# Blocks of 80 rows, 5 for each DMA engine, in place of 64 rows and 4, in a column roll of 8192 x 8192 floats

## Chip, cores, metric

One core of one Trainium2 chip. The metric is the device time in microseconds (us). A profile is a separate execution; its span is about 1.8 us shorter than the time of the same execution (815.4 and 817.17, 838.7 and 840.44). All ratios below are those of the record, worked out from fast runs of the same rounds on one chip, so they are not quite the ratio of the medians quoted beside them; the plain means of the listed runs give the same within 0.001. Intervals are 95%.

## The reference

```python
def setup_inputs():
    return {"x": np.random.randn(8192, 8192).astype(np.float32), "shift": 100}

def reference(x, shift):
    return np.roll(x, shift, axis=1)
```

Nothing is computed. Each row of 32 KiB moves 100 columns to the right, and the last 100 columns come to the front.

## The kernel before

A row is cut in two. The **long piece**, output columns 128 to 8191, is 8064 floats or 32,256 bytes, and goes straight from HBM (the chip's main memory) to HBM. The **head piece**, output columns 0 to 127, goes through on-chip memory; GpSimd issues it, and the change does not touch it.

```python
engines = [nc.sync, nc.scalar]
...
xm = x.rearrange("(c e j) w -> j e c w", e=16, j=4)
om = out.rearrange("(c e j) w -> j e c w", e=16, j=4)
depth = n_rows // 64 // 4
for c in range(4):
    for j in range(4):
        if a < n_cols:
            cs = slice(c * depth, (c + 1) * depth)
            engines[j % 2].dma_start(out=om[j, :, cs, a:], in_=xm[j, :, cs, g:n_cols - s])
...
for k, h in enumerate(tiles):          # head pieces, after loads and copies
    for q in range(Q):
        nc.gpsimd.dma_start(out=ot[k, q, :, :, :a], in_=h[:, q])
```

In a copy `j` is fixed, `e` is the outermost dimension and deals the rows to the 16 DMA engines (the traces list the queue of a packet, not its engine), and `c` steps from block to block. Row `64c + 4e + j` is engine `e`'s. So neighbouring engines stand 4 rows or 128 KiB apart (I call this the **pitch**), and an engine's next row in the same copy lies 64 rows or 2 MiB further on (the block step). SyncE and ScalarE each issue 8 such copies, 32 rows deep for each engine.

## Time and profile before

| | before |
|---|---|
| median of the timed runs | 828.96 us (828.69 to 829.57) |
| span of the profiled execution | 815.4 us |
| bytes read plus written in HBM | 536.9 MB |
| busy time of VectorE, GpSimd | 3.7 us, 16.1 us |
| shortest, median hold of one long row by an engine (470 to 800 us) | 1.19, 1.53 us |

No compute engine matters. The useful number is one that the page does not print for a stretch: the HBM traffic. The prediction works it out from the megabytes of the DMA queues and shows the lines. (q1 and q10 are the two hardware queues, q0 is the software queue.)

### The profile page before, as it was taken

How to read it: one execution, taken by the hardware profiler on the slowest of the kernel's cores; microseconds unless marked ns; L12 is line 12 of the kernel's file. 1: busy time of each engine (PE TensorE's matmuls, PEld its weight loads, DVE VectorE, ACT ScalarE, POOL GpSimd, SP SyncE). 2: the span in 40 equal slices, each digit the busy share in tenths (PEclk: the TensorE clock that was granted, in tenths of full speed). 3: DMA queues.
4: the chain of work that ended last, by engine and by line, in shares of the span. 5: the costliest groups of instructions: out<-in, count | busy, mean ns of one | idle time of the engine just before them, and what ended most of it. 6: DMA issues, size and time to landing. Idle time of an engine off the chain costs nothing. (4 is left out here: it accounts for less than half of the span.)

```text
span 815.4 us, 93 instructions
## 1 busy us (share of the span) xinstructions
DVE 3.7 (0%) x4; POOL 16.1 (2%) x22
## 2 busy tenths in 40 slices
DVE  0000000000000000000000000000000000000000
POOL 3000001000010000000000000000000000000000
DMA  9999999999999999999999999999999999999996
GB/s 310 341 328 347 330 349 335 337 340 346 338 337 346 338 348 348 347 333 345 340 344 337 349 326 335 334 329 334 335 329 331 329 335 334 332 331 332 329 334 250
DMA packets 10784, 272.63 MB, mean 334 GB/s; under 512 B 544, under 2 KB 544, under 8 KB 2592
## 3 DMA queue, kind: packets, MB, share of 16 engines
q10 hardware_dynamic: 4224, 132.12, 47.0%
q1 hardware_dynamic: 4224, 132.12, 46.9%
q0 software_dynamic: 2336, 8.39, 4.5%
HBM read 268.44 MB, written 268.44 MB: 658 GB/s over the span
## 5 line engine op out<-in xcount | busy, mean ns | idle before, releaser
L76 POOL DMA_DIRECT2D out_dram<-h x8 | 6.9, 954 | 170.1 <-DMA h<-in_x_dram 144.1
L67 POOL DMA_DIRECT2D t<-in_x_dram x6 | 5.4, 910 | 0.8 <-PEq L107 0.8
L69 DVE COPY h<-t 128x2400 f32<-128x2400 f32 x2 | 2.8, 1410 | 208.5 <-DMA t<-in_x_dram 208.5
L71 POOL DMA_DIRECT2D h<-in_x_dram x2 | 1.8, 883 | 28.6 <-DMA t<-in_x_dram 28.6
L68 POOL DMA_DIRECT2D h<-in_x_dram x2 | 1.8, 882 | 27.0 <-DMA t<-in_x_dram 27.0
L72 DVE COPY h<-t 128x672 f32<-128x672 f32 x2 | 1.0, 503 | 0.0
L93 POOL MEMSET const-float32-0.0<- 128x1 f32 x1 | 0.1, 99 | 0.2 <-issue 0.2
L93 POOL MEMSET const-bfloat16-1.0<- 128x1 bf16 x1 | 0.1, 103 | 0.0
L93 POOL MEMSET const-float32-1.0<- 128x1 f32 x1 | 0.1, 99 | 0.0
L93 POOL MEMSET const-uint8-127<- 128x1 uint8 x1 | 0.1, 99 | 0.0
## 6 DMA issues: line engine op xcount, KB each, us to landing
out_dram<-in_x_dram SPq DMA_DIRECT2D x8, 16128.0 KB, 401.3
out_dram<-in_x_dram ACTq DMA_DIRECT2D x8, 16128.0 KB, 400.5
out_dram<-h POOLq DMA_DIRECT2D x8, 512.0 KB, 182.5
t<-in_x_dram POOLq DMA_DIRECT2D x6, 512.0 KB, 118.2
h<-in_x_dram POOLq DMA_DIRECT2D x2, 400.0 KB, 151.3
h<-in_x_dram POOLq DMA_DIRECT2D x2, 112.0 KB, 146.1
```

The costliest lines, as they stand in the source:

```text
L67: nc.gpsimd.dma_start(out=t[:, q - 1], in_=lead)
L68: nc.gpsimd.dma_start(out=h[:, Q - 1, :, :s], in_=xt[k, Q - 1, :, :, n_cols - s:])
L69: nc.vector.tensor_copy(h[:, :Q - 1, :, :s], t[:, :, :, :s])
L71: nc.gpsimd.dma_start(out=h[:, 0, :, s:], in_=xt[k, 0, :, :, :g])
L72: nc.vector.tensor_copy(h[:, 1:, :, s:], t[:, :, :, s:])
L76: nc.gpsimd.dma_start(out=ot[k, q, :, :, :a], in_=h[:, q])
L93: nc = _bacc.Bacc("TRN2", target_bir_lowering=False, num_devices=1)
```

## The change

The likely intent: engines and blocks at steps that are no power of two, so that the 16 streams do not fall on the same parts of HBM. The block grows to 80 rows, the pitch to 160 KiB and the block step to 2.5 MiB. As 8192 is not a multiple of 80, 32 rows are left for one more copy; and as 5 is odd, copies fall to the two queues by a running number.

```diff
-    xm = x.rearrange("(c e j) w -> j e c w", e=16, j=4)
-    om = out.rearrange("(c e j) w -> j e c w", e=16, j=4)
-    depth = n_rows // 64 // 4
-    for c in range(4):
-        for j in range(4):
+    V = 5
+    blocks = n_rows // (16 * V)
+    top = blocks * 16 * V
+    xm = x[:top].rearrange("(c e j) w -> j e c w", e=16, j=V)
+    om = out[:top].rearrange("(c e j) w -> j e c w", e=16, j=V)
+    n = 0
+    for c0 in range(0, blocks, 26):
+        for j in range(V):
             if a < n_cols:
-                cs = slice(c * depth, (c + 1) * depth)
-                engines[j % 2].dma_start(out=om[j, :, cs, a:], in_=xm[j, :, cs, g:n_cols - s])
+                cs = slice(c0, min(c0 + 26, blocks))
+                engines[n % 2].dma_start(out=om[j, :, cs, a:], in_=xm[j, :, cs, g:n_cols - s])
+                n += 1
+    if top < n_rows and a < n_cols:
+        nc.sync.dma_start(out=out[top:, a:].rearrange("(c e) w -> e c w", e=16),
+                          in_=x[top:, g:n_cols - s].rearrange("(c e) w -> e c w", e=16))
```

## The prediction

> **What bounds the kernel now.** I read the page's header and its 40 slices first, then its DMA queues, then the chain, then the table of stretches and the DMA view of two stretches.
>
> ```profile
> span 815.4 us, 93 instructions
> DMA  9999999999999999999999999999999999999996
> DMA packets 10784, 272.63 MB, mean 334 GB/s; under 512 B 544, under 2 KB 544, under 8 KB 2592
> q10 hardware_dynamic: 4224, 132.12, 47.0%
> q1 hardware_dynamic: 4224, 132.12, 46.9%
> q0 software_dynamic: 2336, 8.39, 4.5%
> HBM read 268.44 MB, written 268.44 MB: 658 GB/s over the span
> another core or an unknown queue 24%; DMA 4%; POOL 1%; issue 0%; POOLq 0%; PEldq 0%
> ```
>
> The reader is to see that the DMA engines are 90% busy or more in every slice but the last, that the two hardware queues (the long row pieces, issued from SyncE and ScalarE) hold 94% of the engines' time, and that the chain of waits is of no use here: it names the GpSimd side, which the timeline shows issuing its last transfer at 241.7 us of 815, and the long copies never appear in it. So the limit is the transfers. The question is which part of them: the 16 engines, or the HBM that they read and write. Busy engines do not decide it, because an engine that waits for memory counts as busy. Two stretches do, one with all three queues and one with the long pieces alone:
>
> ```profile
> DMA packets 6394, 141.06 MB, mean 341 GB/s; under 512 B 385, under 2 KB 385, under 8 KB 2259
> q10 hardware_dynamic: 2129, 66.61, 46.3%
> q1 hardware_dynamic: 2134, 66.77, 45.1%
> q0 software_dynamic: 2131, 7.68, 8.4%
> ...
> DMA packets 3498, 109.57 MB, mean 332 GB/s; under 512 B 101, under 2 KB 101, under 8 KB 101
> ```
>
> A long piece goes HBM to HBM, so each byte is read and written there; a head piece has one end in on-chip memory and counts once. From 10 to 424 us that gives 2 x (66.61 + 66.77) + 7.68 = 274.4 MB in 414 us, 663 GB/s. From 470 to 800 us it is 2 x 109.57 = 219.1 MB in 330 us, 664 GB/s. The mix differs, the engines' rate differs (341 and 332 GB/s), the HBM rate does not. Now the end:
>
> ```profile
> core 0: us, DVE busy (x) POOL busy (x), PEclk, DMA share, GB/s
> ...
> 470.00:800.00 330.00, 0.00 (x0) 0.00 (x0) 1.00 0.99 332
> 800.00:806.00 6.00, 0.00 (x0) 0.00 (x0) 1.00 0.79 323
> 806.00:812.00 6.00, 0.00 (x0) 0.00 (x0) 1.00 0.59 253
> 812.00:815.40 3.40, 0.00 (x0) 0.00 (x0) 1.00 0.07 28
> ```
>
> While all engines work, one moves 332 / (0.99 x 16) = 21.0 GB/s. With 21% of their time gone an engine moves 323 / (0.79 x 16) = 25.6, and with 41% gone 253 / (0.59 x 16) = 26.8. Losing a fifth of the engines cost 3% of the rate. The packet records say the same: a 32,256 byte row holds its engine 1193 ns at the least (27.0 GB/s), 1534 ns in the median of 470 to 800 us, and 1194 ns for every row that starts after 806 us. So an engine could do a row in 1.19 us, and 512 rows in 611 us; it takes longer because together they run into about 664 GB/s of reads plus writes. **That plateau is the bound.** The whole sum: 536.9 MB / 664 GB/s = 808.5 us, plus about 7 us of beginning and end at a lower rate, is the span of 815.4; the timed 828.96 lies 13.6 us above the span.
>
> **What the Trainium skill says.** "DMA: Bandwidth & Descriptors", section "Specifications", gives about 27 GiB/s for one engine and 716 GB/s for an HBM stack. The fastest rows here (27.0 GB/s) lie somewhat below the first, and 664 is 93% of the second, so the trace agrees that HBM is nearly full. The same page, "Latency and other measured facts", row "HBM row pitch at large powers of two", has copies between HBM tensors at 207 GB/s for a pitch of 512 KiB, 164 for 2 MiB and 103 for 4 MiB, and about 214 once 4 KiB is added; it calls channel aliasing an inference. This is the likely reason for the change. The pitch between engines is 4 rows x 32 KiB = 128 KiB now and 160 KiB after, between blocks 2 MiB and 2.5 MiB. The trace doesn't show such a loss: 329 GB/s in each direction is above the page's undisturbed figure. Section "Issuing engines are not separate DMA queues" says that SyncE and ScalarE feed the same engines; the trace agrees, since both queues move 132.12 MB in the same time. "Why a DMA increments its semaphore by 16 and not by 1" takes the number of engines of a copy from the outermost dimension, 16 here before and after.
>
> **The change, part by part.**
> 1. Bytes and rows: none is added. 8192 = 102 x 80 + 32, so an engine gets 102 x 5 + 2 = 512 rows, as before 128 x 4 = 512. Rows stay whole packets of 32,256 bytes. Worth 0 us.
> 2. Issues: 20 copies and a tail of 32 rows in place of 16. Each adds 16 completion records of 4 bytes; the records show 9 ns for one. 5 more are 80 records, 5 per engine, 0.05 us. An issue's own time lies beside running transfers: an issuing instruction of some 84 us is one that waits for room. A copy is 26 rows deep for each engine in place of 32, so the eight in flight still leave each engine 78 or more rows in its two queues. Worth under 0.1 us.
> 3. Share of the queues: SyncE takes even numbers and the tail, (3+2+3) x 26 + 2 x 24 + 2 = 258 rows for each engine; ScalarE (2+3+2) x 26 + 3 x 24 = 254. ScalarE's queue ends 4 rows earlier. A row alone on an engine took 1194 ns after 806 us, so a single queue fills it. Worth 0 to 1 us.
> 4. The uneven end: from 800 us on the engines run out one after another, the stretches above hold 323 x 6 + 253 x 6 + 28 x 3.4 = 3.55 MB, which 332 GB/s would move in 10.7 us of the 15.4. So 4.7 us is all that a perfect end could give. Today engine e always sits at the same offset modulo 2 MiB (e x 128 KiB plus j rows); after the change the offsets wander with the block, so a lasting disadvantage of one engine may even out. I estimate 0 to 3 us of gain.
> 5. Address pattern, the purpose: if banks or channels collide because of the fixed offsets, the plateau rises. Everything else stays. I estimate +0 to 0.5% of rate, 0 to 4 us.
> Sum: 829 - 1.5 - 2 + 0.5 = 826 us.
>
> **The rivals.**
> First, **aliasing is real** and the new pitch lifts the plateau. 2% of time needs 16.6 us, so a rate of 664 x 808.5 / 791.9 = 678 GB/s, 95% of the stack's figure; at 690 the time would be 829 - 30 = 799. For it: 77 to 85% of the rows take longer than the 1.21 us of an undisturbed one, and reads and writes at like offsets could meet in one bank. Against it: collisions should slow rows also below the plateau, but at 646 GB/s (800 to 806 us) an engine reached 95% of its own best rate, and the plateau was the same at 10 us, with the engines just started in step, as at 700 us, where they have drifted apart. It does not refute a loss tied to the fixed offsets, for those do not change with drift.
> Second, **the fixed offsets were an advantage**: 16 engines at 16 different multiples of 128 KiB never share one; wandering offsets coincide by chance. If the plateau fell by 3% to 644, the span's 808.5 would become 834 and the time 854. Nothing in the trace speaks for it beyond the neat layout.
> Third, **a copy or queue runs dry**, through unequal copies of 24 and 26 rows or the tail behind the last. It would cost at most the 4 rows, 4 x 1.2 = 5 us, time 834. The depth in flight speaks against it.
> Fourth, the engines become the bound: not with a row at 1.19 us where 1.53 is the median.
>
> **Range and chances.** Most likely nothing that matters moves: the bound is bytes through HBM and the bytes stay. A plateau between 655 and 677 makes 840 and 813; with the end and the queues, 810 to 840 should hold it 8 times in 10. Faster by over 2% (under 812.4) needs a plateau above 678, near the stack's figure: 0.12. Slower by over 2% (over 845.5) needs one below 651: 0.08. Within 2%: 0.80.
>
> **What would show it.** Queue of SyncE about 133.2 MB in 258 x 16 + 11 x 16 = 4304 packets, of ScalarE 131.1 MB in 4224; landing of a long copy near 401 x 26 / 32 = 326 us, since eight are in flight either way; head pieces as before. Step 5 is right if bytes counted as above give 660 to 668 GB/s in the middle of the span; step 4 if the last 15 us hold more than 3.55 MB. The prediction is wrong if that rate leaves 651 to 678, or if the hardware queues show engines idle in the middle.

## The result and the profile after

| | before | after |
|---|---|---|
| median, same rounds | 828.83 us (4 runs) | 841.08 us (4 runs) |
| ratio | | 1.0151 [1.0128, 1.0175] |
| span of the page | 815.4 us | 838.7 us |

The change costs 1.5%. That is within 2%, which had a chance of 0.80, but 1 us above the range. A warning first: the two pages lie 23.3 us apart and the timed runs only 12.3. The page of before is of an execution of 817.17 us, while its timed runs took about 829. Later rounds explain the kind of difference: on four chips the same kernel took 818 to 822 us in the median, on a fifth 832. So these two pages give the place of the loss, but its size has to come from kernels run on one chip (runs e1 and e2 below).

The header, the DMA lines and the HBM line of the page after:

```profile
span 838.7 us, 98 instructions
DMA  9999999999999999999999999999999999999996
GB/s 297 327 325 329 321 328 332 324 327 334 341 316 337 340 331 330 335 336 327 340 339 335 323 322 318 326 326 326 323 326 317 328 323 328 320 325 325 329 317 252
DMA packets 10864, 272.63 MB, mean 325 GB/s; under 512 B 624, under 2 KB 624, under 8 KB 2672
q10 hardware_dynamic: 4224, 131.09, 47.3%
q1 hardware_dynamic: 4304, 133.15, 47.0%
q0 software_dynamic: 2336, 8.39, 4.4%
HBM read 268.44 MB, written 268.44 MB: 640 GB/s over the span
```

The bytes are the same, the engines are as busy, and the rate is lower in nearly every slice. Neither queue runs dry. Packets and megabytes of the two queues are those of the prediction's third step. The same two stretches of the DMA view as in the prediction, first 10 to 424 us, then 470 to 800 us, each with its queues (packets, MB, share of 16 engines):

```profile
DMA packets 6207, 136.74 MB, mean 330 GB/s; under 512 B 385, under 2 KB 385, under 8 KB 2198
q10 hardware_dynamic: 2066, 64.58, 46.7%
q1 hardware_dynamic: 2072, 64.74, 44.8%
q0 software_dynamic: 2069, 7.43, 8.3%
...
DMA packets 3452, 106.87 MB, mean 324 GB/s; under 512 B 137, under 2 KB 137, under 8 KB 139
```

The first holds 2 x (64.58 + 64.74) + 7.43 = 266.1 MB in 414 us, 643 GB/s, where before had 663. The second holds 2 x 106.87 = 213.7 MB in 330 us, 648 GB/s, where before had 664. **The plateau itself is lower**, by 3.1% and 2.5%. At 648 GB/s the 536.9 MB take 828.5 us in place of 808.5, 20 of the 23.3 us between the two pages.

The end, from the table of stretches of the kernel after (length, VectorE, GpSimd, clock, DMA share, GB/s):

```profile
core 0: us, DVE busy (x) POOL busy (x), PEclk, DMA share, GB/s
823.30:829.30 6.00, 0.00 (x0) 0.00 (x0) 1.00 0.85 296
829.30:835.30 6.00, 0.00 (x0) 0.00 (x0) 1.00 0.54 231
835.30:838.70 3.40, 0.00 (x0) 0.00 (x0) 1.00 0.11 47
```

The last 15.4 us hold 296 x 6 + 231 x 6 + 47 x 3.4 = 3.32 MB, worth 10.3 us at 324 GB/s, so 5.1 us are lost where before lost 4.7. The end neither gave nor took anything that counts.

### The profile page after: what moved, and what is told of

It is laid out like the page before. It is cut to its first block, busy times and chain, and to the rows that moved or that the text cites. A ratio compares the mean times of both kernels' runs of the same rounds, so it can differ in the third digit from the quotient of the medians.

```text
span 838.7 us, 98 instructions
## 1 busy us (share of the span) xinstructions
DVE 3.7 (0%) x4; POOL 16.1 (2%) x22
```

## Experiments

The theory that I formed from this: **the address pattern of the 5-row blocks lowers the rate that HBM gives** (A), either because an engine's offset now wanders from block to block (A1) or because of the 160 KiB pitch itself (A2). The rival: the new form of issuing, more and shallower copies and another deal to the queues (B). In all kernels the head pieces are unchanged. Only the lines of the long pieces are shown.

### Which part of the change

**e1**: the changed code with 4 rows for each engine.

```diff
-    V = 5
+    V = 4
```

> Blocks of 64 rows and 4 for each engine as before, but issued by the changed code: copies 26 and 24 deep in place of 32, 20 of them, queues taken in turn by a running number. Theory A (the address pattern of 5 rows lowers the plateau of HBM traffic): time within 0.4% of the kernel before, ratio 0.996 to 1.004. Rival B (the shallower copies, their number and the way they fall to the two queues): ratio 1.010 to 1.018, like the changed kernel.

Measured: 820.75 us against 818.48, ratio 1.0023 [1.0001, 1.0045].

**e2**: the changed kernel again, on the same chip and in the same rounds.

> The changed kernel itself, to have it on the same chip and in the same rounds as its variants. All theories: ratio 1.013 to 1.018 to the kernel before, plateau of reads plus writes near 648 GB/s between 470 and 800 us. If it comes out under 1.008, the 1.5% depended on the chip or on where the arrays lay.

Measured: 832.66 us, ratio 1.0173 [1.0145, 1.0200]. B is out: the issue form is worth about 0.2%, the 5 rows about 1.5%. (e1 has no tail copy of 32 rows; neither has e3 below, which loses as much as e2, so the tail is not the cause.) The DMA view of 470 to 800 us, first of e1, then of e2:

```profile
DMA packets 3529, 109.51 MB, mean 332 GB/s; under 512 B 134, under 2 KB 134, under 8 KB 134
```

```profile
DMA packets 3490, 108.45 MB, mean 329 GB/s; under 512 B 128, under 2 KB 128, under 8 KB 128
```

Doubled and divided by 330 us: 663.7 and 657.3 GB/s, 1.0% less, and not the 648 that e2's expectation gave. The earlier stretch, 10 to 424 us, is worse. Its queues (packets, MB, share of 16 engines), first of e1, then of e2:

```profile
q10 hardware_dynamic: 2139, 66.54, 46.6%
q1 hardware_dynamic: 2148, 66.71, 45.2%
q0 software_dynamic: 2143, 7.72, 8.2%
```

```profile
q10 hardware_dynamic: 2098, 65.58, 46.8%
q1 hardware_dynamic: 2103, 65.54, 44.6%
q0 software_dynamic: 2097, 7.54, 8.4%
```

The sums are 274.2 and 269.8 MB in 414 us, 662 and 652 GB/s, 1.6% less. The two losses make 414 x 1.6% = 6.7 us and, over the remaining 390 us, 3.8 us: 10.5 of the 12.7 us between their spans (815.7 and 828.4).

**e3**: pitch still 5 rows, but a copy steps 320 rows (10 MiB), so an engine keeps its offset modulo 2 MiB within a copy. 192 rows go in four small copies of the old form.

```diff
-    xm = x[:top].rearrange("(c e j) w -> j e c w", e=16, j=V)
+    xm = x[:8000].rearrange("(c o e j) w -> o j e c w", o=4, e=16, j=5)   # out likewise; one copy for each (o, j)
```

> Pitch between engines still 5 rows (160 KiB), but each copy steps 320 rows (10 MiB, a multiple of 2 MiB) instead of 80, so an engine keeps its offset modulo 2 MiB within a copy, as in the kernel before; 192 rows are left to four small copies of the old form. Theory A1 (offsets that wander by block let engines that have drifted apart meet at the same offset): the loss goes, ratio 0.995 to 1.005. Theory A2 (the 160 KiB pitch between the engines itself): ratio stays 1.012 to 1.020.

Measured: 835.11 us, ratio 1.0205 [1.0185, 1.0224]. Holding the offset in place does not give the loss back. A1 as the whole cause falls. (The step of 10 MiB is tried in no other run; that it costs nothing of itself is not shown.)

**e4**: blocks of 80 rows, but the first 64 dealt 4 to an engine and the last 16 one to an engine.

```diff
-    xm = x[:top].rearrange("(c e j) w -> j e c w", e=16, j=V)
+    xb = x[:8160].rearrange("(c b) w -> c b w", b=80)                      # out likewise
+    x4 = xb[:, :64].rearrange("c (e j) w -> j e c w", j=4)                 # j = 0..3
+    x1 = xb[:, 64:].rearrange("c e w -> e c w")                            # the fifth copy
```

> Blocks of 80 rows stepped by 2.5 MiB as in the changed kernel, but within the block the first 64 rows are dealt 4 to an engine (pitch 128 KiB) and the last 16 rows one to an engine. Theory A1 (wandering block offsets): ratio 1.012 to 1.020, like the changed kernel. Theory A2 (the pitch between engines): four fifths of the copies run as before, ratio 1.000 to 1.006. Rival B: 1.010 to 1.018.

Measured: 825.13 us, ratio 1.0077 [1.0053, 1.0100], between the two expectations. With e3 it speaks for A2: with most of the old pitch back, more than half of the loss is gone. What is left is not cleared up. e1 gives 0.2% to the issue form, and a fifth of the 0.9% that e11 below finds for a pitch of one row is another 0.2%; the other 0.4% may be the wandering step. On the page of e4 the rate is 657 GB/s from 10 to 424 us and again from 470 to 800 us: what came back, against e2, came back in the first stretch only.

### The pitch varied

**e5 to e8**: the changed code with other numbers of rows.

```diff
-    V = 5
+    V = 8     # e5;  3 in e6, 2 in e7, 6 in e8; copies 32, 29, 32 and 29 deep
```

> 8 rows for each engine, blocks of 128: pitch between engines 256 KiB, again a power of two. Theory A2a (the engines do best when their offsets agree modulo a large power of two): within 0.5% of the kernel before. Rival A2b (the wider the pitch the worse): at least as slow as with 5 rows, ratio 1.015 to 1.04. Aliasing as I had it in the prediction: slower than 4 rows too.

> 3 rows for each engine, blocks of 48 and a tail of 32 rows: pitch 96 KiB, not a power of two but narrower than before. A2a: ratio 1.010 to 1.025, like 5 rows. A2b: 0.99 to 1.00, faster than or like 4 rows.

> 2 rows for each engine, blocks of 32: pitch 64 KiB. A2a with a bound at 128 KiB: slower, ratio 1.005 to 1.02. A2a for any power of two: ratio within 0.5% of 1. A2b: 0.985 to 1.00.

> 6 rows for each engine, blocks of 96 and a tail of 32 rows: pitch 192 KiB = 3 x 64 KiB. A2a: ratio between those of 4 and 5 rows or like 5 rows, 1.005 to 1.02. A2b: 1.017 to 1.03, above 5 rows.

Measured, against 821.82 us in the same rounds: 8 rows 822.78 us, 1.0027 [0.9998, 1.0057]; 3 rows 828.64 us, 1.0096 [1.0069, 1.0124]; 2 rows 823.47 us, 1.0037 [1.0005, 1.0070]; 6 rows 826.41 us, 1.0072 [1.0034, 1.0109]. "The wider the worse" is out: 8 rows beat 3. The powers of two lie within 0.4%, the others lose 0.7 to 1.0%, but the intervals of 2 and 6 rows overlap. In these kernels the block step changes with the pitch (it is 16 times the pitch); e3 and e4 move the one without the other.

**e11 and e12**: two pitches that tell apart what makes a power of two good.

```diff
+    xm = x.rearrange("(c h e) w -> h e c w", e=16, h=2)               # e11: pitch 1 row, a queue for each h
+    xm = x[:8064].rearrange("(c e j) w -> j e c w", e=16, j=12)       # e12: pitch 12 rows, 128 rows in the old form
```

> 1 row for each engine: pitch 32 KiB, the smallest power of two, with the two queues on neighbouring groups of 16 rows. If engines must agree in the low offset bits (a multiple of 64 or 128 KiB): the worst, ratio 1.01 to 1.02, like 3 and 5 rows. If any power of two will do: 0.998 to 1.006.

> 12 rows for each engine, blocks of 192 rows and the last 128 rows in the old form: pitch 384 KiB = 3 x 128 KiB, so the 16 engines stand at the same 16 offsets modulo 2 MiB as with 4 rows, only in another order. If only the set of offsets modulo 2 MiB counts: ratio 0.997 to 1.005. If the pitch has to be a power of two at higher bits also: 1.007 to 1.02, like 3 and 6 rows.

Measured, against 821.11 us: 1 row 827.45 us, 1.0089 [1.0052, 1.0125], so not any power of two will do. 12 rows 824.83 us, 1.0056 [1.0034, 1.0077]. This lies between its two expectations (up to 1.005, from 1.007), and the interval reaches into both; e12 decides nothing.

**e13 to e15**: wide pitches.

```diff
+    xm = x.rearrange("(b e h c) w -> b h e c w", e=16, h=2, c=32)           # e13: pitch 64 rows = 2 MiB
+    xm = x[:7680].rearrange("(b e h c) w -> b h e c w", e=16, h=2, c=40)    # e14: pitch 80 rows = 2.5 MiB
-    V = 5
+    V = 16                                                                  # e15: pitch 512 KiB, copies 32 deep
```

> Each engine copies its own run of 64 neighbouring rows, so the pitch between engines is 2 MiB and all 16 stand at the same offset modulo 2 MiB while in step. Collision theory (engines at equal offsets modulo 2 MiB meet in one bank or channel; also what the Trainium skill's row on HBM pitch suggests): ratio 1.05 or more. If the address bits above 2 MiB spread them as well as those below: 0.995 to 1.01.

> The same with 80 neighbouring rows for each engine, pitch 2.5 MiB = 5 x 512 KiB, and 512 rows in the old form at the end. Collision theory: faster than the 2 MiB pitch, ratio 1.00 to 1.02. Theory that an odd factor in the pitch is what costs: slower than the 2 MiB pitch by 0.8 to 1.5%.

> 16 rows for each engine, pitch 512 KiB: four offsets modulo 2 MiB, each shared by four engines. Collision theory: 1.02 or more. Odd-factor theory: 0.997 to 1.006, like 2, 4 and 8 rows.

Measured, against 821.47 us: 2 MiB 1430 to 1553 us (the fastest: 1430.07 / 821.47 = 1.74); 2.5 MiB 829.27 us, 1.0105 [1.0074, 1.0137]; 512 KiB 863.80 us, 1.0510 [1.0492, 1.0529]. The HBM line of the page of e13, with its DMA line, then of e14, then of e15:

```profile
DMA  9999999999999999999999999999999999999998
...
HBM read 268.44 MB, written 268.44 MB: 376 GB/s over the span
```

```profile
HBM read 268.44 MB, written 268.44 MB: 648 GB/s over the span
```

```profile
HBM read 268.44 MB, written 268.44 MB: 622 GB/s over the span
```

The DMA line of e13 is as full of nines as any other while the traffic is 376 GB/s: busy engines say nothing on their own. A long row of e13 held its engine 2.68 us in the median (470 to 800 us), against 1.53 before. Engines 2 MiB apart do hinder each other: e14 has the form of e13 (but for its last 512 rows) and another pitch, and the loss is nearly gone. But "the offset modulo 2 MiB" is not the whole rule. At 2.5 MiB the 16 engines have only four such offsets, as at 512 KiB, and lose 1% instead of 5%. My expectation for e14 had not counted that. One reading is that address bits above 2 MiB help to spread the engines. It is not shown, as e14 and e15 differ in the step too: in a copy of e14 an engine's next row is the neighbouring one, in e15 it lies 8 MiB further on. For the same reason e15 does not tell whether its 5% come from the pitch of 512 KiB or from the step of 8 MiB.

**e16**: pitch 4 rows, but SyncE copies the upper half of the matrix and ScalarE the lower.

```diff
+    xm = x.rearrange("(u c e j) w -> u j e c w", u=2, e=16, j=4)            # queue u
```

> 4 rows for each engine as before, but SyncE copies the upper half of the matrix and ScalarE the lower, 128 MiB apart, instead of neighbouring rows. If the neighbourhood of the two queues' rows matters: outside 0.995 to 1.005. If only the pitch between engines matters: within it. Under 0.98 it would be a version that beats both kernels; I do not expect that.

Measured: 819.67 us against 821.47, ratio 0.9978 [0.9963, 0.9993]. That the rows of the two queues were neighbours does not matter. It beats the kernel before, but by 0.2%.

### Reads or writes

A copy moves a row to the same row, so one side's order can only be changed alone if rows go to wrong places. **e9 and e10**: their outputs were wrong; every row is read once and written once.

```diff
-  out=om[j, :, cs, a:],             in_=xm[j, :, cs, g:n_cols - s]
+  out=om4[j4, :, c4:c4 + d, a:],    in_=xm5[j5, :, c5:c5 + d, g:n_cols - s]    # e9:  read by fives, written by fours
+  out=om5[j5, :, c5:c5 + d, a:],    in_=xm4[j4, :, c4:c4 + d, g:n_cols - s]    # e10: read by fours, written by fives
```

> Wrong on purpose: the rows are read in the order of the 5-row blocks and written in the order of the 4-row blocks (all rows once, same copies). Control of what side it is. If the loss comes from the reads: ratio 1.013 to 1.020 and a plateau near 650. If from the writes: 0.998 to 1.005 and a plateau near 664. If it needs both sides at the same offsets: near 1.00 for this and the next run.

> Wrong on purpose, the mirror of the run before: read in the order of the 4-row blocks, written in the order of the 5-row blocks. If the loss comes from the writes: ratio 1.013 to 1.020. If from the reads: 0.998 to 1.005. If each side has its share: both runs near 1.008.

Measured, against 821.11 us: e9 830.87 us, 1.0128 [1.0108, 1.0149]; e10 823.19 us, 1.0027 [1.0009, 1.0046]. The 5-row order costs on the read side; on the write side there is nothing beyond the 0.2% of the issue form. Whether the reads are all of it is not shown: e9 is just below its expected 1.013 and 0.4% short of e2, which ran on another chip. The DMA view of 470 to 800 us of e9 and of e10 points the same way, though less clearly (658 and 662 GB/s):

```profile
DMA packets 3492, 108.51 MB, mean 329 GB/s; under 512 B 128, under 2 KB 128, under 8 KB 128
```

```profile
DMA packets 3518, 109.25 MB, mean 331 GB/s; under 512 B 131, under 2 KB 131, under 8 KB 131
```

From 10 to 424 us the difference is larger: 648 GB/s in e9 and 657 in e10, worked out as before.

**e17 and e18**: the same split at the pitch of 2 MiB, also wrong.

```diff
+  out=om4[...],  in_=xp[...]      # e17: read at 2 MiB, written by fours
+  out=op[...],   in_=xm4[...]     # e18: read by fours, written at 2 MiB
```

> Wrong on purpose: rows read at the pitch of 2 MiB between engines, written in the order of the 4-row blocks. If reads collide and writes hardly do: most of the slow time, over 1250 us. If the writes are what collides: near 825 us. If both sides: in between, 1000 to 1250 us.

> Wrong on purpose, the mirror: rows read in the order of the 4-row blocks, written at the pitch of 2 MiB. Reads alone: near 825 us, under 870. Writes alone: over 1250 us. Both: 1000 to 1250 us.

Measured, on the chip where the kernel before took 831.80 us: e17 1062.09 us in one run (the other, 1079.15), e18 1022.67 us, 1.2304 [1.2235, 1.2374]. Both sides collide at 2 MiB, reads somewhat more as far as one run shows. "Reads alone" holds for the 5-row order and is no general rule.

## Why the prediction was wrong

**The bound** was right. The engines are held by HBM traffic at a plateau, and the loss is a lower plateau.

**Steps 1 to 3** (bytes, issues, queues) came out as told: packets and megabytes to the last one, and e1 puts the whole issue form at 0.2%, or 2 us (its interval reaches from 0.1 to 3.7), against the under 1.1 us that I had. The long copies landed after 337 to 339 us, where I had said 326.

**Step 4** ("I estimate 0 to 3 us of gain" from the uneven end) failed: the end lost 5.1 us in place of 4.7.

**Step 5** is the step that failed: "if banks or channels collide because of the fixed offsets, the plateau rises ... I estimate +0 to 0.5% of rate". It fell, by 1.6% early and 1.0% later where both kernels ran on one chip. The sum of the prediction took 2 us off for this step (the middle of its 0 to 4 us) and should have added about 12 (1.5% of 829). On the pages the rate left the 651 to 678 that I had set as the sign of being wrong: 643 and 648. The sign was wrong because I took a power of two to be the harmful case. With 16 engines at a pitch of 128 KiB it is not: 2, 4 and 8 rows are the best pitches measured, and the harm of a power of two begins between 8 rows (256 KiB, 1.0027) and 16 (512 KiB, 1.0510).

**The rivals.** The second, "the fixed offsets were an advantage", had the direction. The size it gave, a plateau of 644, is near the 643 and 648 of the pages by luck: on one chip e2 had 652 and 657, and the time came to 841 us and not to 854. Its mechanism is only half right: e3 kept the offsets fixed within a copy and lost as much, so the pitch costs without any wandering; what the wandering adds is open (e4). I gave slower by over 2% only 0.08, which the result does not contradict; that the time stayed within 2% (0.80) is no credit to step 5, whose sign was wrong. And I pressed the upper end of the range to 840 by treating both directions of step 5 as about equal and small. Nothing in the trace of before could have given me that: one pattern was running in it. My argument that rows near the plateau ran at 95% of their best rate was made with 12.6 engines working and on the old pattern, so it said nothing of the new one.

**One reading was wrong outright**: "the timed 828.96 lies 13.6 us above the span" is no overhead. The profiled execution itself took 817.17 us, and the rest is a difference between executions, probably between chips, as the kernel before took 818 to 832 us on the five chips of the experiments.

**What stays open**: which address bits choose the part of HBM, hence why 5 rows are worse than 3 or 6; why the 5-row order hurts on the read side alone; what the remaining 0.4% of e4 is; and why chips differ. That engines meet in the same channel or bank may be the reason, but it is not shown: no record in a trace names a channel or a bank, and with 5 rows no two engines stand at equal offsets modulo 2 MiB while in step.

## What to carry to other kernels

When DMA engines are busy all the time, work out the HBM bytes per second in two stretches with a different mix. If the rate is the same, as the 663 and 664 GB/s here, memory is the likely bound, and the bytes and the address pattern are what to look at. The distance between the 16 engines' streams is then a setting to be swept, not reasoned out: here powers of two from 64 to 256 KiB were best, pitches with an odd factor cost 0.6 to 1.7%, 512 KiB (with a step of 8 MiB) cost 5% and 2 MiB three quarters. And compare profiles only of runs on one chip, for the same kernel differed by up to 1.6% from chip to chip, as much as the effect under study.

## What the Trainium skill lacked or had wrong

- "DMA: Bandwidth & Descriptors", section "Latency and other measured facts", row on the HBM row pitch: it begins at 512 KiB. The runs add the range below it for 16 engines copying HBM to HBM: time ratios 1.0089 at 32 KiB, 1.0037 at 64, 1.0023 at 128, 1.0027 at 256, and 1.0096, 1.0173, 1.0072 and 1.0056 at 96, 160, 192 and 384 KiB (on three chips; the block step changes too). A reader who takes from the row that powers of two are to be avoided goes wrong here.
- The same row has 207 GB/s at 512 KiB and 164 at 2 MiB where 214 is full, losses of 3% and 23%. In this case's pattern the HBM rate over the span fell from 658 to 622 GB/s (5%) and to 376 (43%). The direction agrees, the size depends on the pattern.
- The row does not say which side collides. At 2 MiB reads alone gave 1062.09 us and writes alone 1022.67, with the kernel before at 831.80.
- The 214 GB/s in each direction that the row calls full is no ceiling for copies from HBM to HBM: from 470 to 800 us the kernel before moved 332 in each direction, 664 of reads plus writes, 93% of the 716 that the section "Specifications" of the same page gives for a stack.
- No page consulted says that chips differ: the same kernel took 818.48, 821.11, 821.47, 821.82 and 831.80 us in the median on five of them, each in one session, so that chip and session are not told apart.
